# A hybrid attention and state-space layer on one core: two token blocks side by side over each tile of a head's weights, and a shorter pause between chunks of the recurrence

## The chip, the core and the metric

The kernel runs on one core of one Trainium2 chip. The metric is the device time of one execution in microseconds (us). An execution with the profiler on gives, beside its time, a trace of every instruction. The core has a matrix engine (TensorE: PE for its matmuls, PEld for the loads of the stationary operand), a vector engine (VectorE, DVE), a scalar engine (ScalarE, ACT), a general engine (GpSimd, POOL) and a queue that issues the transfers (SyncE, SP). Each of them takes its instructions in the order in which the program lists them.

## What is computed

One layer for 1024 tokens of width 1024, all in float32:

```
h = RMSNorm(x)
[q | k | v | z_a | xBC | z_s | dt | gate_logits] = h @ w_in
A: differential attention, 8 heads: two softmax maps per head (q, k of 64 columns each, RMS-normed),
   their difference times v (128 columns), per-head RMSNorm, times silu(z_a)
B: Mamba-2 recurrence, 32 heads in 4 groups, state 128, chunks of 128 tokens:
   causal convolution on xBC, chunked scan, grouped RMSNorm(y * silu(z_s))
merged = sigmoid(g_a) * (y_a @ w_proj_attn) + sigmoid(g_s) * (y_s @ w_proj_ssd)
out = x + merged @ w_out
```

## The kernel before

**Matmuls.** Every float32 operand of a large matmul is split into a high and a low part of a faster matmul type, `hi = round(x)` and `lo = x - hi`, and a product is three matmuls: hi by hi, hi by lo, lo by hi (`steps3`, L625 to L631, which gives control back after each). The normed input lies transposed in two resident tiles, `hH` and `hL`, as 8 slices of 128 features by 1024 tokens.

**Stages.** The front (convolution inputs, gates, z, dt) comes first. It is followed by `att_proj` (L797) for each of the 8 heads in turn, then by the last gates, by the products with the projection weights, and by the output product. Attention blocks (`att_block`, L887) and the recurrence (`ssd_core`, L1402) run in among the projections: a head's attention starts once its first four token blocks are projected, and the recurrence starts in the front and goes on through the heads.

**The projection of a head.** Its weights are 8 tiles of 128 features by 512 columns: 128 each of q, k, v and z_a. For each of 8 blocks of 128 tokens, `att_proj` takes one of the 8 PSUM banks (tile `pma`) and `proj_tok` (L760) runs over the 8 weight tiles, with three matmuls of 512 columns for each: 24 matmuls per block, 192 per head. The token slice of `hH` or `hL` is the stationary operand, the weight tile moves. `w_need` (L608) holds the projection back until the planner's time for the tile has come. The last block gives each weight tile's buffer back (`w_done`, L614). After a block, `att_evac` (L820) empties the bank: ACT takes squares of q and k, tanh of z_a and a copy of v; DVE sums the squares; POOL makes the reciprocal roots (`rsqrt`, L263); DVE multiplies q and k by them into a `qk` tile, one for two blocks, out of at most four (`qkm`). The bank is free after that. Four blocks on, `qk_stack` (L840) transposes q and k on PE (tile `pq`).

**The supply of weights.** A weight tile is loaded by SP into one of four `raw` buffers, copied to its high part by ACT (L463) and subtracted by DVE, or for every third tile by POOL (L465), into one of nine `w` buffers. A head holds eight of the nine until its last token block. So the next head's tiles come in while that last block runs and after it.

**The recurrence.** `ssd_core` starts a chunk (`ssd_chunk`, L1436), pauses for `PACE` us of the planner's clock (for `SLOW`, 40 us, before the heads when buffers are short), and starts the next one when the chunk two before it has finished (L1426). There are 8 chunks in each of 4 groups, 32 in all. Per chunk, PE makes four transposes of the input (tile `px`), small products (`pc`, `pb`), state products (`pO`, `pS`) and four transposes of the result (`py`); most steps between them are on ACT and DVE.

**The order of the work.** A planner in the program (`Plan`, L81) writes every engine's list when the program is built. It keeps a clock for PE and one for each other engine, with a cost for each operation. The projections and products are the bulk, one matmul at a time; everything else is tasks with due times. A task that is due goes ahead of the bulk (`run`, L118), and the bulk fills PE otherwise. Where the bulk waits for a weight tile and no task is due, the planner moves its clock forward and PE's list has nothing to put there. On the chip each engine then follows its list and waits by semaphores for what is really late.

```
def w_need(i):
    while i not in w_at:
        yield pl.t + 0.1
    while w_at[i] > pl.t:
        yield w_at[i]
...
while c - state["n"] >= 2 or c and c - 1 not in state["did"]:
    yield pl.t + 0.2
pl.spawn(ssd_chunk(g, c, state, abs_))
yield pl.t + (PACE if bigs.avail(3) <= pl.t or 'setup' in ready else SLOW)
```

Of the kernel before, what the change touches and what calls it, by code (L numbers as in the profile page):

```python
# [15 lines left out]
P = 128  # L16
S = 1024
D = 1024
KB = D // P
NT = S // P  # L20
# [11 lines left out]
C_DT = 9216  # L32
C_GATE = 9248
NBIG, NW, NRAW, NMID, NSM = 17, 9, 4, 16, 8
PACE = 21
FRONT, SLOW = 12, 40.0
FRONT_ORDER = "z0 d0 z1 c16 c20 g0 c0 c2 g2 z2 c4 c6 g4 c18 c22 g6 z3 c8 c10 g8 c12 c14 g10"
PLAIN = (("z", 0),)
# [103 lines left out]
def tile_hybrid_layer(ctx: ExitStack, tc: tile.TileContext, x, norm_w, w_in, q_norm_w, k_norm_w,  # L142
# [28 lines left out]
    pl = Plan()  # L171
    bigs, mids, sms = Slots(NBIG), Slots(NMID), Slots(NSM)
    trs, qlos = Slots(8), Slots(2)
    trs.line = []
    ws, raws = Slots(NW), Slots(NRAW)
    qkm, atm, ytm, smids = Share(mids, 4), Share(mids, 4), Share(mids, 2), Share(mids, 10)
    heads, abb = Share(bigs, 8), Share(bigs, 1)

    def bigt(shape, dt=F32, name="b"):
        return big.tile(shape, dt, tag="b4", name=name)  # L180

    def midt(shape=(P, 512), dt=F32, name="m"):
        return mid.tile(list(shape), dt, tag="b2", name=name)
# [4 lines left out]
    def tin(cols=1, name="t"):  # L188
        return tiny.tile([P, cols], F32, tag=f"t{cols}", name=name, bufs=20 if cols == 1 else 4)
# [4 lines left out]
    mmt = trt  # L194

    def hpt(name):
        return hpool.tile([P, KB, S], F32R, tag="h", name=name)
# [4 lines left out]
    def mm(o, lhsT, rhs, start, stop, after=0.0, **kw):  # L202
        nc.tensor.matmul(o, lhsT=lhsT, rhs=rhs, start=start, stop=stop, **kw)  # L203
        n, m = rhs.free_size(), lhsT.free_size()
        if rhs.dtype == F32:
            c = max(4 * n / 2400, 0.215)
        else:
            c = max(n / 2400 + lag[0], 0.057 if m <= 64 else 0.107)
        pl.t = max(pl.t, after) + c
# [5 lines left out]
    def pe_done():  # L215
        return pl.t + 0.2
# [11 lines left out]
    def act(o, i, f, after, **kw):  # L228
        nc.scalar.activation(o, i, f, **kw)  # L229
        if f in (AF.Silu, AF.Exp) and f != table[0]:  # L230
            table[0] = f
            pl.op("A", 1.3, after)
        c = 0.83e-3 * i.free_size() + (0.052 if in_ps(i) else 0.093) + 0.093 * (("accum_out" in kw) + any(not isinstance(kw.get(i, 0.0), float) for i in ("scale", "bias")))
        return pl.op("A", c, after)
# [9 lines left out]
    def stt(o, a, s, b, op0, op1, after):  # L244
        nc.vector.scalar_tensor_tensor(out=o, in0=a, scalar=s, in1=b, op0=op0, op1=op1)
        sb = not in_ps(a, b)
        return pl.op("V", 0.07 + 0.07 * sb + 1.042e-3 * o.free_size() + (0.0 if isinstance(s, float) else 0.06), after, sb)
# [15 lines left out]
    def rsqrt(dst, src, add, after):  # L263
        cols = src.free_size()
        if isinstance(add, float):
            nc.gpsimd.tensor_scalar(out=dst, in0=src, scalar1=add, scalar2=None, op0=ALU.add)  # L266
        else:
            nc.gpsimd.tensor_tensor(out=dst, in0=src, in1=add, op=ALU.add)
        nc.gpsimd.tensor_tensor(out=dst, in0=dst, in1=mhalf[:, 0:cols], op=ALU.pow)  # L269
        return pl.op("G", 0.55 + 0.18 * cols, after)  # L270
# [21 lines left out]
    hH, hL = hpt("hH"), hpt("hL")  # L292
# [310 lines left out]
    def w_next(n):  # L603
        i = used[0]
        used[0] += n
        return list(range(i, i + n))
# [7 lines that stand above are left out]
    def w_done(i):  # L614
        ws.give(w_slot[i], pl.t + 0.1)
        wts.pop(i)

    def wide(i):
        return wts[i][:, 0].rearrange("p f c -> p (f c)"), wts[i][:, 1].rearrange("p f c -> p (f c)")
# [5 lines left out]
    def steps3(o, a, b, first, last, **kw):  # L625
        mm(o, a[0], b[0], first, False, **kw)
        yield
        mm(o, a[0], b[1], False, False, **kw)
        yield
        mm(o, a[1], b[0], False, last, **kw)  # L630
        yield  # L631
# [128 lines left out]
    def proj_tok(pm, t, ids, last):  # L760
        hb = lambda kb: (hH[:, kb, t * P:(t + 1) * P], hL[:, kb, t * P:(t + 1) * P])
        for kb in range(KB):
            yield from w_need(ids[kb])
            while (t, kb // 4) not in h_at:
                yield pl.t + 0.1
            while h_at[t, kb // 4] > pl.t:
                yield h_at[t, kb // 4]
            yield from steps3(pm, hb(kb), wide(ids[kb]), kb == 0, kb == KB - 1)
            if last:
                w_done(ids[kb])  # L770
# [26 lines left out]
    def att_proj(h):  # L797
        ids = w_next(KB)
        ks = []
        for _ in range(4):  # L800
            ks.append((yield from pl.get(heads)))
        v = bigt([P, NT, P], name=f"v{h}")
        zg = bigt([P, NT, P], name=f"zg{h}")
        kk = [bigt([P, S], F32R, name=f"kk{h}{m}") for m in range(2)]
        hd[h] = (v, zg, kk, ks)
        lefts[h] = [NT, {}]
        qk = []
        for t in range(NT):
            k = yield from pl.get(trs, first=True)
            pm = mmt(f"pma{h}{t}")  # L810
            yield from proj_tok(pm, t, ids, t == NT - 1)
            if t % 2 == 0:
                km = yield from pl.get(qkm)
                qk.append([midt([P, 2, 256], name=f"qk{h}{t}"), km, 0])
            pl.spawn(att_evac(h, t, pm, k, qk[-1][0][:, t % 2, :], qk[-1]), pe_done())
            if t % 4 == 3:
                pl.spawn(qk_stack(h, t // 4, qk), pl.t + 3.0)
                qk = []

    def att_evac(h, t, pm, k, qn, cell):  # L820
        v, zg = hd[h][0:2]
        at = pe_done()
        t2 = act(qn, pm[:, 0:256], AF.Square, at)
        t1 = act(zg[:, t, :], pm[:, 384:512], AF.Tanh, at, scale=0.5)
        tv = act(v[:, t, :], pm[:, 256:384], AF.Copy, at)
        yield t2
        ss = tin(4, "ss4")
        nc.vector.tensor_reduce(out=ss, in_=qn.rearrange("p (a d) -> p a d", a=4), axis=AX.X, op=ALU.add)  # L828
        t2 = pl.op("V", 0.335, t2)
        rs = tin(4, "rs4")  # L830
        yield max(t1, t2)
        t2 = rsqrt(rs, ss, 64 * EPS, t2)
        t1 = stt(zg[:, t, :], zg[:, t, :], 1.0, pm[:, 384:512], ALU.add, ALU.mult, t1)
        yield t2
        t2 = tt(qn.rearrange("p (a d) -> p a d", a=4), pm[:, 0:256].rearrange("p (a d) -> p a d", a=4),
                rs.unsqueeze(2).to_broadcast([P, 4, 64]), ALU.mult, t2)
        trs.give(k, max(t2, tv))
        cell.append(t2)

    def qk_stack(h, half, qk):  # L840
        v, zg, kk, _ = hd[h]
        lo, hi = slice(0, 64), slice(64, P)
        cs = slice(half * 512, half * 512 + 512)
        while len(qk[0]) < 5 or len(qk[1]) < 5 or "consts" not in ready:
            yield pl.t + 0.2
        yield max(qk[0][3:] + qk[1][3:] + [ready["consts"]])
        kq = yield from pl.get(bigs)
        kz = yield from pl.get(qlos)
        qh, ql = bigt([P, 2, 512], F32R, name=f"qh{h}{half}"), qlo[kz]
        done = []  # L850
        for isk in range(2):
            k = yield from pl.get(trs)
            pt = trt(f"pq{h}{half}{isk}")
            for i in range(4):
                tp(pt[:, i * P:(i + 1) * P], qk[i // 2][0][:, i % 2, isk * P:(isk + 1) * P])
            if isk:
                for c in qk:
                    qkm.give(c[1], pl.t + 0.1)
            at = pe_done()
            yield at  # L860
            t1 = at
            for m, (own, other) in enumerate(((lo, hi), (hi, lo))):
                if isk:
                    t1 = act(kk[m][own, cs], pt[own], AF.Copy, at)
                else:
                    act(qh[own, m], pt[own], AF.Copy, at, scale=wqk_c[own])
                    t1 = act(qh[other, m], pt[own], AF.Copy, at, scale=wqk_c[own])
            yield t1
            for m, (own, other) in enumerate(((lo, hi), (hi, lo))):
                if isk:  # L870
                    t1 = tt(kk[m][other, cs], pt[own], kk[m][own, cs], ALU.subtract, t1 - HOP)
                else:
                    t1 = stt(ql[own, m], pt[own], wqk_c[own], qh[own, m], ALU.mult, ALU.subtract, t1 - HOP)
            done.append(t1)
            trs.give(k, t1)
        pl.spawn(att_core(h, half, (qh, ql, kq, kz)), max(done))
# [525 lines left out]
    def ssd_core(g):  # L1402
# [20 lines left out]
        for c in range(NT):  # L1423
# [4 lines left out]
            pl.spawn(ssd_chunk(g, c, state, abs_))  # L1428
            yield pl.t + (PACE if bigs.avail(3) <= pl.t or 'setup' in ready else SLOW)

# [592 lines left out]
```

## Time and profile before

| what | before |
|---|---|
| median of 3 runs | 1604.91 us (1604.36 to 1609.29) |
| the profiled execution: its time | 1603.58 us |
| its span, from the first to the last instruction | 1601.6 us |
| mean granted clock of TensorE | 0.998 |
| busy: PE, DVE, ACT, POOL | 1578.4, 1119.3, 925.9, 749.5 us |

The profiled execution's own time is 1.98 us more than its span, and 1.33 us less than the median of the runs. In the rows of the trace, times are us from the span's start. A row of the stretches gives its two ends, its length, and for each engine the busy time with the number of instructions in brackets; then the granted clock of TensorE as a share of full speed, and the use of the DMA engines. A row of the timeline gives the start, the length, the engine, the line, the operation, the tile written and the tiles read; in square brackets stands how long the engine was idle before and what it waited for. Nearly all PE rows carry L203 or L212, the lines of two helpers, so tiles tell the steps apart.

### The profile page before, as it was taken

Reading aid. Unit: us, or ns where it says so; the run is one execution under the profiler, and the core shown is the slowest. Engines: PE = TensorE matmul, PEld = TensorE weight load, DVE = VectorE, ACT = ScalarE, POOL = GpSimd, SP = SyncE. Lnnn points to the kernel's source line nnn. Section 1 sums busy time; section 2 is a strip of 40 time slices with the busy share of each in tenths; the row PEclk is TensorE's granted clock in tenths of the full one; section 3 lists DMA queues with packets and bytes.
Section 4 is the critical chain, followed back from the end, with each engine's and each line's share of the span. In section 5 each row is a group of like instructions: output and inputs, shape, how many; then the busy total and the mean of one; then the engine's idle time right before and its main releaser. Section 6 shows DMA issues by size and latency. Waiting matters only on the chain.

```text
span 1601.6 us, 25383 instructions
## 1 busy us (share of the span) xinstructions
PE 1578.4 (99%) x8446; PEld 1341.7 (84%) x8446; DVE 1119.3 (70%) x2049; ACT 925.9 (58%) x2239; POOL 749.5 (47%) x882
## 2 busy tenths in 40 slices
PE   8999999999999999999999999999999999999999
PEld 6898889888988888888878888888888888888887
DVE  7967674878567756777777777777566677898831
ACT  8444455665565556667677777687666655352310
POOL 3554455554645534445574645455656424222000
PEclk9999999999999999999999999999999999999999
DMA  5233354344354451414372423334435479698941
GB/s 181 93 109 86 119 155 124 113 133 151 109 144 139 125 175 50 119 46 143 112 233 86 146 80 119 93 99 139 135 114 189 137 242 312 213 336 256 328 145 67
DMA packets 229670, 236.04 MB, mean 147 GB/s; under 512 B 15255, under 2 KB 167584, under 8 KB 229538
## 3 DMA queue, kind: packets, MB, share of 16 engines
q1 hardware_dynamic: 229538, 234.41, 46.4%
q8 instruction: 67, 1.10, 0.3%
q14 instruction: 65, 0.53, 0.1%
HBM read 163.96 MB, written 70.39 MB: 146 GB/s over the span
## 4 chain that ended last, share of the span: by engine, by line
PE 85%; ACT 6%; POOL 3%; DVE 2%; DMA 2%; issue 1%; SPq 0%; POOLq 0%; DVEq 0%; ACTq 0%
PE pma L203 16%; PE py L203 6%; PE fYc L203 6%; PE po L203 5%; PE px L203 4%; PE pz L203 4%; PE fXc L203 4%; PE fZc L203 4%; PE pO L203 4%; PE av L203 3%; PE sc L203 3%; PE tyz L203 3%; PE fYg L203 3%; PE pg L203 3%; PE txz L203 2%; PE fZg L203 2%
## 5 line engine op out<-in xcount | busy, mean ns | idle before, releaser
L203 PE MATMUL pma<-w,hH 128*128 128x512 f32 x1024 | 344.2, 405 | 1.1 <-POOL w L237 0.5
L203 PEld LDWEIGHTS pma<-w,hH 128*128 128x128 f32 x1024 | 187.6, 189 | 35.3 <-ACT at L229 1.4
L203 PE MATMUL pma<-w,hL 128*128 128x512 f32 x512 | 206.1, 403 | 0.0
L237 POOL TENSOR_TENSOR rawf<-rawf,rawf 128x512 f32<-128x512 f32 x54 | 70.1, 1299 | 114.7 <-issue 41.5
L203 PEld LDWEIGHTS pma<-w,hL 128*128 128x128 f32 x512 | 96.9, 189 | 16.9
L229 ACT ACTIVATE p<-p,nm 128x512 f32<-128x512 f32 (+7 forms) x128 | 98.6, 772 | 14.9 <-DVE nm L903 10.2
L203 PE MATMUL fYc<-ft,wp 128*128 128x512 f32 x432 | 105.0, 390 | 0.0
L229 ACT ACTIVATE w<-raw 128x512 fp32r<-128x512 f32 (+1 forms) x98 | 60.7, 626 | 60.3 <-PE po L203 22.9
L203 PEld LDWEIGHTS fYc<-ft,wp 128*128 128x128 f32 x432 | 80.9, 188 | 16.7
L229 ACT ACTIVATE wp<-rawp 128x512 fp32r<-128x512 f32 x72 | 44.3, 627 | 82.3 <-POOL rawp L237 23.7
L229 ACT ACTIVATE wp<-rawf 128x512 fp32r<-128x512 f32 x108 | 64.8, 625 | 43.7 <-POOL rawf L237 19.1
L237 POOL TENSOR_TENSOR w<-raw,w 128x512 fp32r<-128x512 f32 (+1 forms) x30 | 39.2, 1308 | 94.6 <-ACT w L229 79.6
L203 PEld LDWEIGHTS av<-v,at 128*128 128x128 f32 x576 | 73.5, 193 | 7.4 <-ACT at L229 3.4
L229 ACT ACTIVATE ab<-ab,nac 128x128 f32<-128x128 f32 x256 | 78.4, 393 | 1.1 <-POOL ab L1412 0.9
L903 DVE CUSTOM_DVE_ANT_0 p<-sc,maskb 128x512 f32<-128x512 f32 (+3 forms) x128 | 72.1, 585 | 9.8 <-PE sc L203 9.6
L266 POOL TENSOR_SCALAR rs<-ss 128x4 f32<-128x4 f32 (+1 forms) x71 | 21.2, 298 | 122.0 <-DVE ss L828 101.9
L203 PE MATMUL av<-v,at 128*128 128x128 f32 x576 | 75.3, 277 | 2.9 <-ACT at L229 2.9
L237 POOL TENSOR_TENSOR rawp<-rawp,rawp 128x512 f32<-128x512 f32 x36 | 52.7, 1475 | 52.3 <-DVE wp L237 37.6
L269 POOL TENSOR_TENSOR rs<-rs,mhalf 128x4 f32<-128x4 f32 (+1 forms) x71 | 73.9, 1041 | 5.9
L203 PE MATMUL sc<-kk,qh 128*128 128x512 f32 (+2 forms) x192 | 66.7, 354 | 0.4 <-DVE kk L237 0.4
L237 DVE TENSOR_TENSOR wp<-rawf,wp 128x512 fp32r<-128x512 f32 x72 | 55.9, 790 | 14.1 <-ACT wp L229 14.0
L237 DVE TENSOR_TENSOR w<-raw,w 128x512 fp32r<-128x512 f32 (+1 forms) x68 | 57.3, 852 | 9.5 <-ACT w L229 9.0
(332 smaller groups left out, 4575.3 us busy)
## 6 DMA issues: line engine op xcount, KB each, us to landing
raw<-in_w_in_dram SPq DMA_DIRECT2D x80, 256.0 KB, 3.1
rawf<-in_w_in_dram SPq DMA_DIRECT2D x72, 256.0 KB, 3.7
ab<-act_d SPq DMA_DIRECT2D x32, 512.0 KB, 4.6
cv_d<-cv SPq DMA_DIRECT2D x48, 256.0 KB, 2.3
t_d<-ts SPq DMA_DIRECT2D x24, 512.0 KB, 3.0
xr<-cv_d SPq DMA_DIRECT2D x32, 256.0 KB, 3.6
zc<-z_d SPq DMA_DIRECT2D x32, 256.0 KB, 3.8
ys_d<-xdt SPq DMA_DIRECT2D x32, 256.0 KB, 2.4
```

What stands on the lines that cost most here:

```text
L203: nc.tensor.matmul(o, lhsT=lhsT, rhs=rhs, start=start, stop=stop, **kw)
L229: nc.scalar.activation(o, i, f, **kw)
L237: (nc.vector if eng == "V" else nc.gpsimd).tensor_tensor(out=o, in0=a, in1=b, op=op)
L266: nc.gpsimd.tensor_scalar(out=dst, in0=src, scalar1=add, scalar2=None, op0=ALU.add)
L269: nc.gpsimd.tensor_tensor(out=dst, in0=dst, in1=mhalf[:, 0:cols], op=ALU.pow)
L903: nc.vector.tensor_tensor_reduce(out=p[:, j:e], in0=sc[i][:, 0:e - j], in1=maskb[:, S - n + j:S - n + e], scale=-1.0, scalar=nms[i - 1] if ...
```

## The change

In `att_proj`, the first two token blocks of each head take two PSUM banks and run side by side: over each weight tile go three matmuls of block 0 and then three of block 1. Blocks 2 to 7 run one after the other as before. The `qk` tile is taken ahead of the block's matmuls and no longer behind them. The wait for the slices of `h` in `proj_tok` is not in the new loop. The pause `PACE` between chunks of the recurrence goes from 21 to 19 us of the planner's clock.

```diff
-PACE = 21
+PACE = 19
...
         qk = []
-        for t in range(NT):
-            k = yield from pl.get(trs, first=True)
-            pm = mmt(f"pma{h}{t}")
-            yield from proj_tok(pm, t, ids, t == NT - 1)
-            if t % 2 == 0:
-                km = yield from pl.get(qkm)
-                qk.append([midt([P, 2, 256], name=f"qk{h}{t}"), km, 0])
-            pl.spawn(att_evac(h, t, pm, k, qk[-1][0][:, t % 2, :], qk[-1]), pe_done())
-            if t % 4 == 3:
-                pl.spawn(qk_stack(h, t // 4, qk), pl.t + 3.0)
+        for ts in ((0, 1), (2,), (3,), (4,), (5,), (6,), (7,)):
+            pms = []
+            for t in ts:
+                k = yield from pl.get(trs, first=True)
+                pms.append((mmt(f"pma{h}{t}"), k))
+                if t % 2 == 0:
+                    km = yield from pl.get(qkm)
+                    qk.append([midt([P, 2, 256], name=f"qk{h}{t}"), km, 0])
+            for kb in range(KB):
+                yield from w_need(ids[kb])
+                for t, (pm, k) in zip(ts, pms):
+                    yield from steps3(pm, hblk(kb, t), wide(ids[kb]), kb == 0, kb == KB - 1)
+                    if kb == KB - 1:
+                        pl.spawn(att_evac(h, t, pm, k, qk[-1][0][:, t % 2, :], qk[-1]), pe_done())
+                if ts[0] == NT - 1:
+                    w_done(ids[kb])
+            if ts[-1] % 4 == 3:
+                pl.spawn(qk_stack(h, ts[0] // 4, qk), pl.t + 3.0)
                 qk = []
+
+    def hblk(kb, t):
+        return hH[:, kb, t * P:(t + 1) * P], hL[:, kb, t * P:(t + 1) * P]
```

## The prediction

> **What bounds the kernel now.** I read the page's engine rows and slices first, then the stretches, then what PE waited for, then the timeline around the two worst head starts.
>
> ```profile
> span 1601.6 us, 25383 instructions
> PE 1578.4 (99%) x8446; PEld 1341.7 (84%) x8446; DVE 1119.3 (70%) x2049; ACT 925.9 (58%) x2239; POOL 749.5 (47%) x882
> PE   8999999999999999999999999999999999999999
> ```
>
> PE is busy for 1578.4 of 1601.6 us. No other engine comes near, so the time is PE's work plus PE's idle time, and all idle time together is 23.2 us, 1.4%. The change adds no matmul and removes none. It can win only idle time, and time in which PE runs slowly.
>
> ```profile
> 240.00:579.20 339.20, 337.03 (x1873) 292.52 (x1872) 235.75 (x376) 199.07 (x387) 170.55 (x148) 1.00 0.45 134
> 579.20:1222.60 643.40, 631.30 (x3601) 538.67 (x3600) 451.29 (x1014) 448.52 (x1331) 357.60 (x545) 0.99 0.37 116
> 592.20:1111.60 519.40, 507.85 (x2926) 434.39 (x2925) 383.43 (x844) 369.06 (x1092) 279.66 (x427) 0.99 0.36 112
> 1111.60:1283.10 171.50, 170.95 (x935) 144.96 (x934) 102.78 (x230) 107.81 (x304) 101.28 (x141) 1.00 0.44 146
> ```
>
> These stretches (length, then busy PE, PEld, DVE, ACT, POOL, then clock) are the front with the recurrence in it; the eight heads, from the first `pma` to the last; the part of them with the recurrence at its quick pace; and the rest up to the products. The heads hold 643.40 - 631.30 = 12.10 us of PE's idle time, and 11.55 us of idle time lies where the recurrence runs. Behind the recurrence there is only 0.55 us. So the two edits act on the one stretch that has something to give.
>
> ```profile
> PE av L203 <- ACT at L229: 2.9, 1, 2.9
> PE pS L203 <- ACT at L229: 2.1, 1, 2.1
> PE px L212 <- DVE qk L237: 1.9, 1, 1.9
> PE pO L203 <- DVE ab L237: 1.5, 3, 1.0
> PE pma L203 <- POOL w L237: 0.5, 2, 0.4
> PE pma L203 <- ACT at L229: 0.5, 2, 0.3
> ```
>
> In the list of what PE waited for in the heads (total, times, longest), only 0.5 us is a direct wait of `pma` for a weight tile. Three single waits make 6.9 us of the 12.10. They are late evacuations by ACT and DVE.
>
> **Part one: two blocks over each weight tile.** The stretches of blocks 0 and 1 of each head, the worst two of the eight and the sum of all eight:
>
> ```profile
> 811.80:837.20 25.40, 22.12 (x120) 17.98 (x119) 17.97 (x29) 18.05 (x51) 21.32 (x26) 0.93 0.81 256
> 901.20:926.00 24.80, 22.64 (x134) 18.72 (x132) 18.45 (x35) 18.71 (x54) 14.62 (x22) 1.00 0.51 148
> ...
> sum 144.00, PE 137.73 PEld 114.04 DVE 95.35 ACT 103.91 POOL 93.79; mean PE 17.22 PEld 14.26 DVE 11.92 ACT 12.99 POOL 11.72
> ```
>
> The first two blocks hold 144.00 - 137.73 = 6.27 us of idle time in 144 us; the other 499.4 us of the heads hold 5.83 us, 1.17%. So head starts idle nearly four times as much as the rest. The worst of them, head 3, on PE and on ACT and SP:
>
> ```profile
> 821.88 0.39 PE L203 MATMUL pma<-w,hL 128*128 128x512 f32 x1
> 822.14 0.33 PE L212 MATMUL pya<-ident,y 128*128 128x128 f32 x1
> 825.33 1.38 PE L203 MATMUL av<-v,at 128*128 128x128 f32 x8 [2.86 <-ACT at L229]
> 826.36 0.77 PE L203 MATMUL pO<-sh,ch 128*128 128x512 f32 x1
> ...
> 829.49 0.30 PE L212 MATMUL pya<-ident,y 128*128 128x128 f32 x1
> ```
> ```profile
> 822.81 0.63 ACT L229 ACTIVATE w<-raw 128x512 fp32r<-128x512 f32 x1 [1.31 <-DMA raw<-in_w_in_dram]
> 824.16 0.63 ACT L229 ACTIVATE w<-raw 128x512 fp32r<-128x512 f32 x1 [0.72 <-DMA raw<-in_w_in_dram]
> 824.69 0.58 ACT L229 ACTIVATE at<-pa 128x512 f32<-128x512 f32 x1
> ```
> ```profile
> 821.57 5.97 SPq L258 DMA_DIRECT2D raw<-in_w_in_dram  x3
> ```
>
> The wait is put down to `at`, but the copy that makes it stands in ACT's list behind two splits of weight tiles, and those waited 1.31 and 0.72 us for loads which SP issued late. The planner had no projection matmuls to put between 822.14 and 825.33, because the head's next weight tile was not there. That is what the change mends. One block needs a new tile every three matmuls, the pair every six.
>
> ```profile
> 36.80 27.91 PE pmz L203 x123
> 117.67 2.72 PE fYc L203 x12
> 579.20:1222.60 643.40, 411.24 (x1536) 276.30 (x1535) 43.64 (x126) 45.11 (x189) 0.99 0.37 116
> ```
>
> The chain's rows give the price of one matmul of 512 columns: 2.72/12 = 0.227 us. The first row holds projections (`pmz`) whose last three blocks already run side by side in three banks, at 27.91/123 = 0.227 us each. So changing banks every three matmuls costs nothing, and the 1536 matmuls of `pma` (last row, those of that tile alone) stay 1536. A tile's work for one block is 3 x 0.227 = 0.68 us; the pair has 1.36 us per tile. The seventh tile, missing at 822, would be wanted after 18 more matmuls, 4.1 us later: more than the gap of 2.86 us. If head starts came to idle like the rest, 1.17% of 144 us or 1.7 us would stay, and 6.27 - 1.7 = 4.6 us would go.
>
> Something goes with it. Behind that gap PE runs at half speed:
>
> ```profile
> 696.45 0.63 PE L203 MATMUL pma<-w,hH 128*128 128x512 f32 x1
> ...
> 698.58 1.43 PE L203 MATMUL av<-v,at 128*128 128x128 f32 x6
> ```
> ```profile
> 826.30:829.50 3.20, 3.20 (x10) 2.42 (x10) 0.00 (x0) 2.59 (x11) 3.04 (x5) 0.50 0.85 247
> 695.60:700.20 4.60, 4.56 (x18) 3.96 (x19) 1.74 (x4) 4.19 (x14) 1.75 (x3) 0.63 0.57 205
> ```
>
> The granted clock is 0.50 after the gap of 2.86 us, and it dips after the 2.10 us gap too (0.63 over that stretch). From 826.36 to 829.49 seven matmuls took 3.13 us, where 7 x 0.227 = 1.59 would do: 1.5 us lost. This goes with the gap, so part one is -6.1 us. The second dip (five matmuls in the 2.13 us from 696.45 to 698.58, 1.0 us lost) lies in head 1's middle blocks and isn't counted.
>
> [...]
>
> What part one adds: a second open bank. Before, a block's bank was open for some 5.4 us (24 x 0.227) of pure `pma`; now two are open for 10.9 us, and both are evacuated at once. POOL's share of that is serial:
>
> ```profile
> 587.25 0.23 POOL L266 TENSOR_SCALAR rs<-ss 128x4 f32<-128x4 f32 x1 [3.73 <-DVE ss L828]
> 587.57 1.05 POOL L269 TENSOR_TENSOR rs<-rs,mhalf 128x4 f32<-128x4 f32 x1
> 612.59 0.60 PE L212 MATMUL pq<-ident,qk 128*128 128x128 f32 x4
> ```
>
> The second bank comes free about 1.4 us later for it (0.23 + 1.05 and the hop). While block 2 runs (5.4 us), five banks instead of six are left for the rest. I price this at nothing, because block 2's own matmuls cover it. Without that cover the price is one wait like `px <- DVE qk`, 1.9 us, per head: 15.2 us, the upper end. The earlier claim of `qk` tiles is covered too: head 0's first two are free again after the transposes at 612.59, and the fifth is wanted at head 1's start, 640.9. `qk_stack` is still spawned behind block 3, so attention starts as before. The wait on `h` that is dropped ended long before the heads.
>
> **Part two: the pause of 19.** Over the tile `px`, four transposes per chunk:
>
> ```profile
> 592.10:1087.60 495.50, 13.92 (x92) 10.84 (x91) 27.57 (x40) 24.98 (x42) 0.99 0.37 112
> 234.70:553.90 319.20, 5.30 (x36) 4.31 (x36) 9.64 (x14) 8.92 (x15) 1.00 0.43 130
> ```
>
> That is 23 chunks in 22 intervals of 22.5 us in the heads, and 9 chunks in 8 intervals of 39.8 us in the front. The quick interval is 1.5 us over its pause of 21: the rule that chunk c-2 must be finished, and the buffers, set some of them. At a ratio of 19/21 it becomes 20.4, and the last chunk starts 44 us earlier; if the rule binds throughout, nothing moves. Ending earlier wins nothing by itself, as only 0.55 us of idle time lies behind it. Denser chunks cost: DVE is at 383.43/519.40 = 74% there and ACT at 71%. PE's idle time per chunk is 2.17/9 = 0.24 us at 39.8 us apart and 11.55/23 = 0.50 at 22.5. On a straight line in chunks per us, 20.4 gives 0.56, or 23 x 0.06 = +1.4 us. The line is crude, since the front has no attention in it. Ends: 0 (the rule binds) and +11.5 (idle time per chunk doubles). A gain is not excluded, as another order may close other gaps, at most the 5.8 us outside the head starts. I take the middle of 0 and 1.4, +0.7, nearest to the row of 22.5.
>
> **Sum.** -6.1 + 0.7 = -5.4 us on the profiled execution's 1603.58, which is 1598.2. The median of the runs lies 1.33 us above that execution, so the median goes from 1604.91 to **1599.5 us**.
>
> **Rivals.** *The gain is given back* (0.26). All order on PE is written anew, and each late evacuation meets another neighbour. If the two-bank evacuation costs a wait of 1.9 us in three of eight heads, 5.7 us return and the time is 1605. For it: three of the waits listed are on evacuations, one of them on `qk` itself. Against: only one wait of `px` on `qk` in eight heads so far.
>
> *Denser chunks make ACT and DVE late* (0.20; slower). Place: `at`, `ab`, `qk` and the weight splits between 592 and 1070. It decides where idle time per chunk passes 0.50 + 4.8/23 = 0.71 us with no gain from the pair; if it doubles, +11.5 us, 1616. For it: the step from 0.24 to 0.50, and splits that already stand in the same ACT list as `at`. Against: both engines keep a quarter of the stretch free, and the pair wants tiles later.
>
> *All that can go, goes* (0.12): the 12.10 us and both clock dips, 2.5: 1590.3. Against: half of that idle time isn't at head starts.
>
> *The pause does nothing* because the rule sets the interval: -6.1 alone, 1598.8; inside my forecast.
>
> **Chances.** The forecast has 0.42, with a range of its own from 1595 to 1602. A run of this kernel can tell about 0.3%, 4.8 us, from no change; 1600.1 is that bound, and my number lies just past it. Faster: 0.34 of the forecast's 0.42 and all of the 0.12, 0.46. Slower: 0.20, and 0.01 of the giving back. Same: the rest, 0.33. The range from 1590 to 1612 reaches from the case in which all goes to the near part of the slower one; it leaves out some 0.12 above and 0.03 below.
>
> **What would show it.** Right: the stretches of blocks 0 and 1 idle near 1 to 2%, no half clock in them, idle time in the heads near 7 us, 1536 `pma` matmuls, the last `px` some 30 to 44 us earlier. Wrong: PE waits `<- DVE qk` or `<- POOL rs` behind the pairs; more idle time per chunk; or an unchanged last `px`. The argument fails if the heads' idle time is as large as before, or lies in new places.

## The result, and the profile after

The median went from 1604.63 to **1595.32 us** (four runs each, 1594.28 to 1596.37 after): a ratio of 0.9941, with a 95% interval from 0.9927 to 0.9956, or 9.3 us less. The forecast was 1599.5 us, 5.4 us less than the median that it started from. The profiled execution took 1594.28 us.

The page of the changed kernel:

```profile
span 1592.6 us, 25370 instructions
PE 1573.6 (99%) x8446; PEld 1338.6 (84%) x8446; DVE 1128.9 (71%) x2049; ACT 924.9 (58%) x2239; POOL 751.4 (47%) x882
```

PE's idle time fell from 23.2 to 1592.6 - 1573.6 = 19.0 us. Its busy time fell by 4.8 us with the same 8446 matmuls. A matmul counts as busy for longer while the granted clock is halved: one of `pma` lists 0.63 us behind the gap in head 1 and some 0.39 us elsewhere. Before its last microseconds the kernel before has two stretches at half clock, here from end to end; the changed kernel has none (a mean of 1.000 over its span).

```profile
696.42:699.83 3.41, 3.41 (x12) 2.91 (x11) 1.74 (x4) 3.22 (x10) 1.38 (x3) 0.50 0.63 238
826.12:829.53 3.41, 3.41 (x12) 2.63 (x11) 0.00 (x0) 2.77 (x11) 3.25 (x5) 0.50 0.85 252
```

At 0.50 of the clock, 3.41 us do the work of 1.7, so the two account for an estimated 3.4 of the 4.8 us. Where the rest comes from was not traced.

The stretches of the changed kernel: the heads, the part with the recurrence at its quick pace, the rest up to the products, the front, and what follows the heads.

```profile
579.20:1209.90 630.70, 625.53 (x3601) 535.86 (x3600) 453.45 (x1013) 446.58 (x1331) 356.06 (x544) 1.00 0.38 118
592.10:1068.40 476.30, 471.57 (x2763) 404.76 (x2762) 364.88 (x798) 349.08 (x1046) 262.46 (x408) 1.00 0.36 112
1068.40:1281.30 212.90, 209.96 (x1131) 177.76 (x1130) 132.49 (x286) 132.44 (x362) 117.83 (x163) 1.00 0.45 148
240.00:579.20 339.20, 336.95 (x1873) 292.43 (x1872) 236.22 (x376) 199.23 (x387) 170.49 (x148) 1.00 0.45 134
...
1209.90:1300.00 90.10, 87.60 (x433) 72.81 (x433) 64.50 (x101) 54.34 (x115) 41.38 (x41) 1.00 0.67 219
```

The front is as it was. The heads idle 5.17 us where it was 12.10. Behind the heads 2.50 us are idle where there was no idle time. Blocks 0 and 1 of the heads, three of the eight and the sum:

```profile
640.10:660.50 20.40, 19.13 (x105) 15.38 (x104) 14.88 (x30) 13.52 (x37) 9.30 (x16) 1.00 0.51 152
...
814.60:831.40 16.80, 16.80 (x93) 13.98 (x92) 13.50 (x23) 13.34 (x31) 16.08 (x19) 1.00 0.93 303
901.00:917.30 16.30, 14.64 (x76) 11.95 (x75) 9.55 (x15) 9.74 (x28) 14.23 (x16) 1.00 0.71 214
...
sum 130.20, PE 126.82 PEld 105.48 DVE 80.81 ACT 91.21 POOL 81.45; mean PE 15.85 PEld 13.19 DVE 10.10 ACT 11.40 POOL 10.18
```

The sum is 130.20 - 126.82 = 3.38 us of idle time where it was 6.27. Head 3 (814.60) no longer idles at all; head 4 (901.00) still loses 1.66 us. Its timeline, and POOL's:

```profile
910.71 0.40 PE L203 MATMUL pma<-w,hH 128*128 128x512 f32 x1
912.76 0.51 PE L203 MATMUL pma<-w,hH 128*128 128x512 f32 x1 [1.66 <-POOL w L237]
```
```profile
911.00 1.71 POOL L237 TENSOR_TENSOR w<-raw,w 128x512 fp32r<-128x512 f32 x1
```

Here the wait has the name that the supply theory gives it. A weight tile's subtraction is the last thing that PE waits for, at a point where the pair could no longer cover it. What PE waited for in the heads, in total:

```profile
PE pma L203 <- POOL w L237: 1.7, 1, 1.7
PE pO L203 <- DVE y L245: 0.7, 1, 0.7
PE av L203 <- ACT at L229: 0.5, 1, 0.5
```

The three long waits of before (2.9, 2.1 and 1.9 us) are all gone, though the one of 2.1 us lay in head 1's middle blocks, which the pair doesn't touch. That is the first sign that more has changed than what the edits act on. The transposes `px`, with their first and last start:

```profile
L212 PE MATMUL px<-ident,xr x128: 270/272/299, 234.6 to 1044.7; 128*128 128x128 f32 x128
```

The last one was at 1087.0, so the recurrence's last chunk starts 42 us earlier. The 22 quick intervals are 452.6/22 = 20.6 us, where 20.4 was forecast.

### The profile page after: what moved, and what is told of

Same layout as the page of the kernel before. It is cut to its first block, busy times and chain, and to the rows that moved or that the text cites. A ratio compares the mean times of both kernels' runs of the same rounds, so it can differ in the third digit from the quotient of the medians.

```text
span 1592.6 us, 25370 instructions
## 1 busy us (share of the span) xinstructions
PE 1573.6 (99%) x8446; PEld 1338.6 (84%) x8446; DVE 1128.9 (71%) x2049; ACT 924.9 (58%) x2239; POOL 751.4 (47%) x882
## 4 chain that ended last, share of the span: by engine, by line
PE 89%; ACT 5%; POOL 2%; DVE 2%; DMA 2%; issue 1%; SPq 0%; DVEq 0%; POOLq 0%; ACTq 0%
PE pma L203 18%; PE py L203 6%; PE fYc L203 6%; PE po L203 5%; PE pO L203 4%; PE px L203 4%; PE pz L203 4%; PE sc L203 4%; PE fXc L203 4%; PE av L203 4%; PE fZc L203 4%; PE tyz L203 3%; PE fYg L203 3%; PE txz L203 2%; PE fZg L203 2%; PE pmz L203 2%
## 5 line engine op out<-in xcount | busy, mean ns | idle before, releaser
L229 ACT ACTIVATE p<-p,nm 128x256 f32<-128x256 f32 (+7 forms) x128 | 98.9, 776 | 36.2 <-DVE nm L914 30.4
L946 POOL TENSOR_TENSOR rec<-s,mone 128x1 f32<-128x1 f32 x64 | 35.9, 563 | 80.2 <-ACT p L229 80.0
```

Source lines behind the costliest of these rows:

```text
L946: nc.gpsimd.tensor_tensor(out=rec, in0=sums[1], in1=mone, op=ALU.pow)
```

## The experiments

The theories as they stood when the runs began. *Supply*: the pair relieves the delivery of weight tiles at head starts, and this is the gain. *Pause*: the shorter pause is the gain. *Order*: any edit to the planner rewrites the order of all engines' lists, and where the long waits fall is then a draw. A fourth, *late sums*, came up on the way.

All kernels in one table. Idle time is the length of a stretch less PE's busy time in it, over blocks 0 and 1 of all heads, and over the rest of the heads' stretch. The clock is the mean granted over the span. These columns come from one profiled execution of each kernel. The medians of e1 to e12 are of 10 to 12 executions (e9: 5), and each ratio below is to the kernel before, timed beside it, with its 95% interval.

| kernel | median, us | blocks 0 and 1 | rest of the heads | clock |
|---|---|---|---|---|
| before | 1604.6 | 6.27 | 5.83 | 0.998 |
| changed: pair, pause 19 | 1595.3 | 3.38 | 1.79 | 1.000 |
| e1: pair, 21 | 1609.0 | 0.54 | 4.23 | 0.996 |
| e2: no pair, 19 | 1607.0 | 6.50 | 8.73 | 0.997 |
| e3: new loop, no pair, 21 | 1602.7 | 4.72 | 3.60 | 0.999 |
| e4: pair on blocks 2 and 3, 21 | 1609.0 | 8.54 | 5.18 | 0.996 |
| e5: pair, 20 | 1606.6 | 0.67 | 13.06 | 0.997 |
| e6: pair, 17 | 1603.1 | 4.92 | 6.36 | 0.999 |
| e7: pair, 21, room for the sums | 1601.0 | 3.04 | 4.43 | 0.997 |
| e8: pair, 19, late sums | 1600.1 | 3.39 | 1.81 | 1.000 |
| e9: pair, 18.8 | 1599.5 | 2.22 | 6.45 | 0.999 |
| e10: pair, 19.2 | 1607.7 | 4.52 | 6.79 | 0.998 |
| e11: no pair, 20.8 | 1607.5 | 12.43 | 4.73 | 0.999 |
| e12: no pair, 21.2 | 1603.1 | 2.47 | 8.34 | 0.998 |

**e1, the pair alone.** The changed kernel with the old pause:

```diff
-PACE = 19
+PACE = 21
```

> The pair over blocks 0 and 1 with the old pause of 21. If the pair relieves the supply of weight tiles at head starts (the prediction's theory), it carries the gain by itself: about 1604.6 - 6 = 1598.5 us, the stretches of blocks 0 and 1 idle no more than 3 us in sum, no half clock. If the gain is the shorter pause's, this run stays at 1604 to 1606. If any new order of the list would have missed the two clock dips by chance, the time may lie anywhere from 1597 to 1606, and head starts idle as much as before (5 to 7 us).

It was slower than before: 1609.0 us, a ratio of 1.0025 (1.0016 to 1.0034). Yet in the heads the pair did what the prediction said. The sum over blocks 0 and 1, the heads, and the products with the end of the second and most of the third:

```profile
sum 124.40, PE 123.86 PEld 103.61 DVE 72.27 ACT 83.82 POOL 75.98; mean PE 15.48 PEld 12.95 DVE 9.03 ACT 10.48 POOL 9.50
...
579.10:1210.80 631.70, 626.93 (x3598) 535.56 (x3598) 452.83 (x1011) 443.63 (x1329) 346.11 (x531) 1.00 0.36 110
...
1380.00:1480.00 100.00, 88.73 (x367) 71.47 (x366) 83.33 (x118) 33.21 (x60) 32.61 (x23) 0.93 0.80 263
```

Blocks 0 and 1 idle 0.54 us, the heads 4.77 us, and the heads end at 1210.8. Then, 170 us later, PE idles 11.27 us in a stretch where it idled not at all before, and half clock comes on top (0.93 over the stretch). What PE waited for after the heads:

```profile
PE py L203 <- DVE u L237: 8.3, 2, 6.0
PE py L203 <- DVE hH L237: 1.9, 1, 1.9
PE py L203 <- DVE hL L237: 1.0, 1, 1.0
```

These are DVE steps of the products. The longest wait, 6.0 us, ends at 1466.5; there `u` stands in DVE's list behind a bunch of splits of the third product's operands. The other wait for `u`, 2.3 us, is behind splits of weights. The operands come from the recurrence's and the attention's results, and from sums of them (`sums_of`, tile `ts`) that POOL makes during the heads and behind them and SP writes out to `t_d`. SP's last such writes in e1, in the changed kernel and in the kernel before:

```profile
1409.84 1.42 SPq L258 DMA_DIRECT2D t_d<-ts  x1
```
```profile
1296.35 0.86 SPq L258 DMA_DIRECT2D t_d<-ts  x2
```
```profile
1342.24 0.38 SPq L258 DMA_DIRECT2D t_d<-ts  x1
```

The theory of *late sums* is: with the pair alone, the heads are over before the sums have had their buffers; with a pause of 19 the recurrence ends earlier and frees them, so the two edits would belong together. The last write alone can't be the sign of it: in the kernel before it comes at 1342.24, and PE doesn't idle in the products there. e7 and e8 test the theory.

**e2, the pause alone.** The kernel before with the new pause:

```diff
-PACE = 21
+PACE = 19
```

> The pause of 19 alone, with the old loop of one block after the other. The prediction's theory: denser chunks cost 0 to 1.4 us, so 1604.6 to 1606, with the head starts' idle time of about 6 us still there. If the pause is what gained: 1595 to 1598. If it is the redrawing of the order: anywhere from 1597 to 1608.

1607.0 us, 1.0012 (1.0002 to 1.0023): 0.3 to 3.7 us slower by the interval, the side that the prediction's line gave. Blocks 0 and 1 idle 6.50 us, as before. So neither edit gains alone, and the 9.3 us are no sum of the two.

**e3, the new loop with single blocks.** Only the order shifts a little:

```diff
-        for ts in ((0, 1), (2,), (3,), (4,), (5,), (6,), (7,)):
+        for ts in ((0,), (1,), (2,), (3,), (4,), (5,), (6,), (7,)):
```

It has the pause of 21, too.

> The new loop with every block by itself and the pause of 21: no pair, only the qk tile taken earlier and the wait on h gone, so that the order of the list shifts a little. This measures what a redrawing of the order alone does. The prediction's theory: no change, 1603 to 1606. If chance is what moves the time, it differs from before by 3 us or more, in either direction.

1602.7 us, 0.9981 (0.9973 to 0.999): 1.9 us faster by the medians and 3.0 by the ratio, with nothing in the program that should gain. The expectation's bound of 3 us for chance is just about met, and "no change" (1603 to 1606) doesn't hold. The heads end early here too, at 1213.6, and PE then idles 3.16 us in the third product, without any pair.

**e4, the pair in the wrong place.** The pause of 21 and

```diff
-        for ts in ((0, 1), (2,), (3,), (4,), (5,), (6,), (7,)):
+        for ts in ((0,), (1,), (2, 3), (4,), (5,), (6,), (7,)):
```

> The pair in the wrong place: blocks 2 and 3 of each head side by side, blocks 0 and 1 one after the other, pause of 21. It has the same two open banks and the same joint evacuation, but the head's weight tiles are all there by then. The prediction's theory: no gain, 1604 to 1606, head starts idle 5 to 7 us in sum. If the gain comes from something else in a pair (fewer evacuations in a row, or a new order), it comes here too: 1596 to 1600.

1609.0 us, 1.0022 (1.0013 to 1.0031). The pair gains nothing there. Blocks 0 and 1, single again, idle more than before:

```profile
812.10:834.50 22.40, 17.82 (x84) 14.32 (x83) 13.48 (x24) 14.15 (x36) 16.32 (x20) 0.92 0.72 221
...
sum 144.80, PE 136.26 PEld 111.91 DVE 88.14 ACT 98.20 POOL 85.03; mean PE 17.03 PEld 13.99 DVE 11.02 ACT 12.28 POOL 10.63
```

**e5 and e6, the pair with pauses of 20 and 17.**

```diff
-PACE = 19
+PACE = 20
```
```diff
-PACE = 19
+PACE = 17
```

> The pair with a pause of 20, between the two. Theory of the late sums: the pair shortens the heads, and the recurrence's end then sets when the sums for the second product can start; with 21 they end at 1410 us and the third product waits 11 us. With 20 the recurrence ends some 20 us earlier than with 21, the last sum lands between 1297 and 1410, and the products wait for less than 11 us: 1594 to 1603 us, heads idle 4 to 6 us. Theory of a redrawn order: no relation with the pause, anywhere from 1594 to 1609.

> The pair with a pause of 17. Late sums: the sums end no later than with 19, products do not wait, and what decides is the heads' idle time with still denser chunks; by the prediction's line at most 1.5 us more, so 1594 to 1598 us. Denser chunks as a cost: heads idle 9 us or more, 1600 or more. If the rule that chunk c-2 must be finished sets the interval already at 19, the last px stays where it is with 19.

e5: 1606.6 us, 1.0017 (1.0009 to 1.0026). The products did not wait at all, so late sums are not the reason here, and the 1594 to 1603 us that they allowed is missed. The heads idle instead, with blocks 0 and 1 nearly free of it:

```profile
sum 143.50, PE 142.83 PEld 120.16 DVE 86.84 ACT 94.72 POOL 72.41; mean PE 17.85 PEld 15.02 DVE 10.86 ACT 11.84 POOL 9.05
...
579.00:1223.90 644.90, 631.17 (x3586) 539.15 (x3585) 452.57 (x1012) 445.80 (x1325) 358.97 (x545) 0.99 0.38 118
```

That is 0.67 us in the first two blocks and 13.06 in the rest. e6: 1603.1 us, 0.9995 (0.9986 to 1.0003), above the 1598 that late sums allowed. The heads idle 11.28 us, as was expected of denser chunks. But the chunks are no denser than with 19:

```profile
L212 PE MATMUL px<-ident,xr x128: 270/272/329, 234.5 to 1045.9; 128*128 128x128 f32 x128
```

The last `px` is where it is with 19, and the heads of the changed kernel idle 5.17 us at the same density. So density can't be the reason for that difference. At 17 something else than the pause sets the interval: the rule that chunk c-2 must be finished, or the buffers. The runs don't tell these two apart.

**e7, room for the sums.** The pair, the pause of 21, and the sums may take buffers sooner:

```diff
-        return 0 if done else 3
+        return 0 if done else 1
```

> The pair with the old pause of 21, and the sums may take a pair of buffers when one is spare instead of three. If the late sums are what made the pair alone slow, this mends it without touching the pause: the last sum lands before 1350 us, the third product does not wait, and the time is 1593 to 1599 us. The price could be buffers missing in attention: heads idle more than 5 us. If the shorter pause is needed for itself, or the gain is chance, it stays at 1604 to 1610.

1601.0 us, 0.9983 (0.9973 to 0.9992): 8.0 us less than e1, to be had without the pause. The last sum is written at 1329.48 and PE idles 0.59 us behind the heads where e1 idled 11.26. The heads took some of it back: they idle 7.47 us where e1's idled 4.77, and there is half clock in them (a mean of 0.84 from 1064.30 to 1085.70). It misses the expected 1593 to 1599 us.

**e8, the sums held back.** The changed kernel, with the sums of the second product held back:

```diff
             while ready.get("ssd", {}).get(g, INF) > pl.t:
                 yield pl.t + 0.5
+            if c == 1:
+                yield pl.t + 40.0
             yield from sums_of(c, range(4))
```

> The changed kernel, pair and pause of 19, but the sums for the second product start 40 us of the planner's clock after the recurrence has ended, about when they start with the pair alone. Late sums: they run into the shortage of buffers again, the last one lands near 1400 us, the products wait for some 5 to 12 us and half clock comes with it: 1601 to 1611 us, with the heads' idle time still about 5 us. If the pause helps in another way, such as a lighter load in the late heads, the time stays within 3 us of 1595.

1600.1 us, 0.9976 (0.9967 to 0.9985), 4.8 us more than the changed kernel. This is the cleanest pair of the study: PE's order is the changed kernel's up to 1113 us, and the idle times of the heads are the same within 0.02 us (3.39 and 1.81 us). The third product's part in e8, and in the changed kernel:

```profile
1405.00:1460.00 55.00, 49.97 (x220) 40.75 (x219) 49.80 (x70) 21.30 (x37) 19.74 (x14) 1.00 0.88 292
```
```profile
1380.00:1480.00 100.00, 100.00 (x443) 82.81 (x442) 92.98 (x136) 40.11 (x70) 26.25 (x19) 1.00 0.86 283
```

5.03 us idle against none, with the last sum written at 1346.91 instead of 1296.35. Late sums are shown as a real cost, of some 5 us here. The half clock that the expectation had with it didn't come (1.00 in the first row), and the time is 1 us below the range. What counts is how many sums are still to come, and not when the last one does. In the ten kernels of the table that write at most one sum behind 1300 us, e4 as late as 1349, PE idles nowhere from 1300 to 1480 us. In e3, e7 and e8, with two, it idles 3.16, 0.59 and 5.03 us; in e1, with four, 11.26.

**e9 to e12, edits of no weight.** The changed kernel with pauses of 18.8 and 19.2, and the kernel before with 20.8 and 21.2:

```diff
-PACE = 19
+PACE = 18.8
```
```diff
-PACE = 19
+PACE = 19.2
```
```diff
-PACE = 21
+PACE = 20.8
```
```diff
-PACE = 21
+PACE = 21.2
```

> The changed kernel with a pause of 18.8 instead of 19: an edit of no weight, which only shifts the planner's due times. If the pair with a pause near 19 is good for a reason of its own, the time stays within 2 us of 1595.3. If the last five microseconds are a lucky order of the list, it goes up by 3 to 12 us, with the idle time coming back outside the first two blocks (there 2 to 13 us in the pairs so far) while blocks 0 and 1 keep to 0.5 to 5 us.

> The same on the other side, a pause of 19.2. Reason of its own: within 2 us of 1595.3. Lucky order: 1598 to 1608 us, blocks 0 and 1 at 0.5 to 5 us of idle time.

> The kernel before with a pause of 20.8 instead of 21. If the order of the list is a draw, it moves by some microseconds from 1604.6, either way (1600 to 1609 us); if not, it stays within 2 us. The theory of the weight supply: blocks 0 and 1 idle 4.5 to 8.5 us, as in all kernels without the pair at the front, whatever the time.

> The kernel before with a pause of 21.2. As with 20.8: 1600 to 1609 us if the order is a draw, 1603 to 1606 if not; blocks 0 and 1 idle 4.5 to 8.5 us in either case.

1599.5 (0.9967, 0.9955 to 0.998), 1607.7 (1.0018, 1.0006 to 1.003), 1607.5 (1.0019, 1.0009 to 1.0028) and 1603.1 us (0.9989, 0.998 to 0.9998). A step of 0.2 us in a pause, which means nothing for the work, moves the changed kernel by +4 and +12 us, and the kernel before by +3 and -1.5. So the order is a draw that moves the time by several microseconds, and the changed kernel is a good one. The sums over blocks 0 and 1 of e10, and of e11 and e12:

```profile
sum 143.40, PE 138.88 PEld 115.95 DVE 93.78 ACT 98.92 POOL 81.04; mean PE 17.36 PEld 14.49 DVE 11.72 ACT 12.37 POOL 10.13
```
```profile
sum 162.10, PE 149.67 PEld 125.83 DVE 112.97 ACT 116.26 POOL 94.90; mean PE 18.71 PEld 15.73 DVE 14.12 ACT 14.53 POOL 11.86
```
```profile
sum 137.60, PE 135.13 PEld 111.17 DVE 92.35 ACT 95.25 POOL 87.36; mean PE 16.89 PEld 13.90 DVE 11.54 ACT 11.91 POOL 10.92
```

e12's 2.47 us falls below the 4.5 that the supply theory gave for every kernel without the pair, and e11's 12.43 lies far above its 8.5. The theory holds on the mean and not for each kernel. Leaving out e8, which shares its heads with the changed kernel, the seven kernels with the pair in front idle 2.8 us in blocks 0 and 1 (0.54 to 4.92), the six without it 6.8 us (2.47 to 12.43). In the rest of the heads the means are 6.2 and 6.1 us: no difference, but a spread from 1.79 to 13.06.

The six kernels that have the pair and differ in the pause alone have a mean of 1603.5 us (1595.3 to 1609.0), the five without a pair (before, e2, e3, e11, e12) 1605.0 (1602.7 to 1607.5). Whether the pair gains time on the mean stays open: 1.5 us is less than either spread. No kernel here beats the changed one.

## Why the prediction was right, and where not

**Blocks 0 and 1.** The prediction put -4.6 us on them. In the changed kernel it was 3.38 - 6.27 = -2.9; over the kernels above it is 2.8 - 6.8 = -4.0. In one kernel that is within the draw, since e12 has 2.47 without a pair; on the mean the pair in front takes the idle time from just there (e1, e5), and in the wrong place it does not (e4).

That the supply of weight tiles is the reason can be read from the gaps. In head 3 of the kernel before, 21 matmuls of `pma` stand ahead of the gap, so the tile missing at 822 was the eighth and not the seventh (with the pair it is wanted 21 matmuls or 4.8 us later, not 4.1). DVE finished it at 824.16, inside the gap:

```profile
823.47 0.69 DVE L237 TENSOR_TENSOR w<-raw,w 128x512 fp32r<-128x512 f32 x1 [0.39 <-ACT w L229]
```

The same can be asked of every gap in blocks 0 and 1 of these 13 kernels: was the head's next weight tile still unfinished when the gap began, or was a tile what `pma` waited for? Such gaps make 4.9 us without the pair in front (0.42 to 10.64) and 0.85 with it (0 to 2.68). All other gaps make 1.9 and 1.8 us. So the whole difference of 4.0 us lies where tiles were missing, as the prediction had it. This is read from the traces; no run changes the supply itself. Two of the three long waits before (2.86 and 1.91 us), listed as late evacuations, began with a tile missing.

**The clock.** The prediction counted 1.5 us for the half clock behind head 3's gap and left out the dip in head 1, 1.0 us by its own working. From end to end each is 3.41 us at 0.50, or 1.7 us. Both are gone. The second is gone because of another order: that gap lay in blocks that the change doesn't touch.

**The pause.** +0.7 was taken, from a straight line through two densities. Pause and pair together gained 13.7 us over the pair alone, and the pause alone lost 2.3. A price per chunk is not what these runs show; the shorter pause moved the whole order and the sums with it. The forecast of the interval, 20.4, was right (20.6). That an earlier end of the recurrence wins nothing by itself was wrong where the pair is in: by the program the second product's sums wait for that end and then for buffers, and room for them took most of e1's idle time in the products away (e7).

**The failing step.** It is the sum, which kept the idle time of the rest of the heads as it was, and left the stretch behind the heads alone. In the changed kernel the rest gave -4.0 us (5.83 to 1.79), and the stretch behind the heads took 2.5 (none before). Together: -2.9 - 4.0 + 2.5 = -4.4 of idle time, near the 4.2 by which the page's idle time fell; PE's busy time gave the other 4.8 us, about 3.4 of it the two stretches of half clock. So the terms gave the direction and about half of the size: 2.9 us and head 3's 1.7 of the 9.0 by which the span fell. The other half is luck, a draw of the order. The prediction had named that draw both ways, as a rival that gives the gain back and as other gaps that may close, at most 5.8 us, and put neither into the sum. e1, e5 and e10 had the bad draw, with the waits in other places than the two banks that the rival blamed.

**The rivals.** The two-bank evacuation didn't show: in the changed kernel no wait of 0.3 us or more in the heads is on `qk` or `rs`. Denser chunks making ACT and DVE late cannot be told from the draw: e2 fits it (15.23 us in the heads), but e6, with the density of the changed kernel, idles 11.28 us there against 5.17.

## What to carry to other kernels

Where a planner writes the order and PE is 99% busy, a change of a few microseconds can't be judged by one kernel: time neighbours that differ in nothing that matters, and take the spread as the error of the comparison. Look at the idle time of the stretch that the edit acts on, since over 13 kernels that told a true effect (4 us) from a draw of 10. Ask of each gap what was missing when it began: the wait that ends it can have another name. And when a stage gets shorter, ask what was prepared under its cover: here the sums for a product 200 us later.

## What the runs showed of the hardware

The length of a gap alone doesn't tell whether the clock falls. Behind a gap of 1.73 us in e7 (first row) it was halved for some 6.8 us: the mean over the 21.40 us from 1064.30 to 1085.70 is 0.84, and 0.16 x 21.40 / 0.50 = 6.8. Behind two gaps in e8, of 2.52 us (second row) and of 2.51 us up to 1457.06, it stayed full, at 1.00 over the 55 us from 1405 to 1460.

```profile
1070.66 0.33 PE L212 MATMUL pya<-ident,y 128*128 128x128 f32 x1 [1.73 <-DVE y L245]
```
```profile
1416.19 0.94 PE L203 MATMUL py<-hL,wp 128*128 128x512 f32 x3 [2.52 <-DVE u L237]
```

In the kernel before, the two stretches at 0.50 last 3.41 us each, and their starts, 696.42 and 826.12, are 129.70 us apart, 38 times 3.41. The 3.41 us ahead of each of them, at full clock, hold 3.41 - 1.30 = 2.11 and 3.41 - 0.79 = 2.62 us of idle time:

```profile
693.01:696.42 3.41, 1.30 (x6) 0.77 (x5) 1.84 (x3) 3.35 (x10) 0.00 (x0) 1.00 0.70 192
822.71:826.12 3.41, 0.79 (x7) 0.80 (x8) 1.75 (x5) 2.54 (x6) 3.25 (x5) 1.00 1.00 342
```

In e7, 3.41 us at full clock with 1.61 us idle (first row) stand ahead of 3.41 us at 0.50 (second row):

```profile
1069.05:1072.46 3.41, 1.80 (x13) 1.67 (x14) 2.94 (x6) 1.49 (x5) 3.25 (x5) 1.00 0.87 252
1072.46:1075.87 3.41, 3.41 (x15) 3.12 (x15) 1.65 (x3) 0.61 (x2) 3.08 (x6) 0.50 0.93 184
```

So the clock fell here behind a gap of 1.73 us and stayed full behind one of 2.52. What decides it beside the length was not shown.
